# Stick-breaking weights without their last product: value differences in place of values

## The chip, the cores and the metric

One core of a Trainium2 chip runs the whole program: two decoder layers over 1024 tokens of width 1024, in float32. The metric is the device time of one execution in microseconds (us), as the median of several runs. PE is TensorE (matrix products and transposes), DVE is VectorE, ACT is ScalarE, POOL is GpSimd, and SP is the engine whose queue issues the DMAs here.

## The reference, cut to what matters

Each layer has three token mixers side by side (stick-breaking attention with 4 heads of 64, multi-head latent attention "MLA" with 4 heads, RWKV-7 with 8 heads), an output projection with a layer norm, and a gated convolutional feed-forward part (FFN). The change touches the first mixer alone:

```python
def stick_breaking_attention(q, k, v):
    scale = q.shape[-1] ** -0.5
    kpos = jnp.arange(s_len, dtype=jnp.int32)
    def block(qb, start):                      # 128 queries
        z = jnp.einsum('bhqd,bhkd->bhqk', qb, k).astype(jnp.float32) * scale
        qpos = start + jnp.arange(Q_BLOCK, dtype=jnp.int32)
        past = kpos[None, :] < qpos[:, None]
        log_keep = jnp.where(past, jax.nn.log_sigmoid(-z), 0.0)
        log_later = lax.cumsum(log_keep, axis=3, reverse=True) - log_keep
        w = jnp.where(past, jnp.exp(jax.nn.log_sigmoid(z) + log_later), 0.0)
        return jnp.einsum('bhqk,bhkd->bhqd', w.astype(v.dtype), v)
```

With b = sigmoid(z) and K[j] = the product of (1 - b) over all past keys from j on, the weight of key j is b[j] * K[j+1], which is K[j+1] - K[j].

## The kernel before, in words

The program is written with a tile framework. It emits instructions in program order with priorities (PRIORITY, lines 45 to 57); a list scheduler then fixes one static order for each engine and puts in the semaphores. A tile tag with `bufs=n` has n buffers in rotation, and a new tile of the tag waits until one of them is free. All DMAs are issued by SP, in their static order, so that one whose wait isn't over holds up those behind it.

A layer runs through these stages:

- `phase_a` (line 1075): the input projections of MLA and RWKV, the RWKV preparations, then the RWKV chain (`rw_chain`), a recurrence over 8 steps for each of two groups of heads. During the second group `proj_sb` (line 263) computes the six projections of the stick-breaking heads, two heads at a time: queries and keys of pair 0, queries and keys of pair 1, then values of pair 0 and of pair 1. After each of the six, `step` lets the chain emit one step more. Each projection is 48 matmuls, evicted by ACT into a tile "pst" (one tag with 4 buffers) and stored to DRAM (`sqd`, `skd`, `svd`). The values are transposed first, 128 by 128 (line 281), through PSUM tiles that the chain uses too (`ps2`: "pa", "py", "pq"), and copied by DVE (line 282) into another "pst" tile.
- The attention (lines 1191 to 1212): four MLA heads and four stick-breaking heads, as four generators whose blocks of 128 queries are interleaved by STREAM_ORDER. Pairs of heads are taken in turn; the second pair goes through its blocks from the longest to the shortest. Four MLA blocks are emitted ahead, before the pools of the chain close (line 1201). The queries and keys come back from DRAM into "pst" tiles (lines 359, 360, 533, 534) and are split into high and low parts.
- `oproj` (output projection, from the last query block to the first) and `ffn`.

A stick-breaking block over LL = 128 to 1024 keys (`stick_block`, `stick_post`): PE computes scores in one or two PSUM pieces (lines 388, 389), ACT takes the tanh (390), POOL fills the diagonal block with -1 where the key isn't past (396), DVE computes (1 - tanh)/2, the factors 1 - b (397), into one of three buffers `kp3` (the tags "LA", "T", "pd" of an earlier stage, cleared by POOL at line 1198), takes their running product from the right (399), and multiplies (1 + tanh) by that product (400). PE transposes the result (339), ACT evicts it (340), and when both heads of a pair have a block, PE multiplies it by the values (`attn_out`, 323), ACT evicts with the factor 0.5 (418), and SP stores it. An MLA block has its own chain of DVE and ACT instructions (maximum 562, 564, 566; exponential 567 on ACT; normalization 580, 582).

Of the kernel before, what the change touches and what calls it, by code (L numbers as in the profile page):

```python
# [69 lines left out]
class Body:  # L70
    def __init__(self, ctx, tc, a):
        self.ctx, self.tc, self.nc, self.a = ctx, tc, tc.nc, a
        self.n = 0
        self.ptags = {}
        self.rot = 0
        self.sq = 0
        self.sn = self.kn = 0
        self.pairs = {}
# [184 lines left out]
    def proj_sb(self, l, pool, step):  # L263
        nc, W = self.nc, self.a["w_in"][l]
        for j in range(2):
            for base, dst in ((SBQ, self.sqd), (SBK, self.skd)):
                hi, lo = self.wload(W, [(base + j * P, P)])
                d = self.t(pool, [P, S], "pst", bufs=4)
                self.proj_copy(hi, lo, d)
                nc.sync.dma_start(dst[j], d)  # L270
                step(4)
        for j in range(2):
            hi, lo = self.wload(W, [(SBV + j * P, P)])
            d = self.t(pool, [P, S], "pst", bufs=4)
            self.proj_copy(hi, lo, d)
            o = self.t(pool, [P, S], "pst", bufs=4)
            for q in range(2):
                pt = self.ps2()
                for i in range(4):
                    ii = 4 * q + i  # L280
                    nc.tensor.transpose(pt[:, i * P : i * P + P], d[:, ii * P : ii * P + P], self.ident)
                nc.vector.tensor_copy(o[:, q * 512 : q * 512 + 512], pt)
            step(4)
            nc.sync.dma_start(self.svd[j], o.rearrange("p (i v) -> p i v", v=P))

# [31 lines left out]

    def attn_out(self, wts, nb, V, av):
        ms = []
        for j in range(nb):  # L320
            for hp in range(2):
                hc = slice(hp * 64, hp * 64 + 64)
                ms.append(self.nc.tensor.matmul(av[hc], V[:, j, hc], wts[hp][:, j, :], start=j == 0, stop=j == nb - 1))
        self.in_order(ms)
# [18 lines left out]
    def stick(self, wp, ip, hp):  # L343
        for pr in range(2):
            if hp == 0:
                self.sv = self.t(wp, [P, NT, P], "mv")
                self.nc.sync.dma_start(self.sv, self.svd[pr])
            V = self.sv
            qk = self.stick_qk(wp, pr, hp)
            for i in range(NT)[:: 1 - 2 * pr]:  # L350
                self.stick_block(i, pr, hp, qk, V, wp, ip)
                yield

    def stick_qk(self, wp, pr, hp):
# [20 lines left out]
    def stick_block(self, i, pr, hp, qk, V, wp, ip):  # L375
# [6 lines left out]
        n = self.sn = self.sn + 1  # L382
        self.kn += 1
        kp = self.kp3[self.kn % 3]
        for u, (a0, a1) in enumerate(self.pieces(LL)):
# [4 lines left out]
            nc.scalar.activation(be[:, a0:a1], s, AF.Tanh, scale=0.0625)  # L390
        self.stick_post(be, kp, i, LL, nb, n, V, hp, pr, wp)

    def stick_post(self, be, kp, i, LL, nb, n, V, hp, pr, wp):
        nc = self.nc
        dg = be[:, i * P : LL]
        nc.gpsimd.affine_select(out=dg, in_=dg, pattern=[[-1, P]], base=0, channel_multiplier=1, compare_op=ALU.is_gt, fill=-1.0)
        nc.vector.tensor_scalar(kp[:, : LL - 1], be[:, 1:LL], -0.5, 0.5, op0=ALU.mult, op1=ALU.add)
        kv = kp[:, : LL - 1][:, ::-1]
        nc.vector.tensor_tensor_scan(kv, kv, self.ones.to_broadcast([P, LL - 1]), 1.0, op0=ALU.mult, op1=ALU.mult)
        nc.vector.scalar_tensor_tensor(be[:, :LL], be[:, :LL], 1.0, kp[:, :LL], op0=ALU.add, op1=ALU.mult)  # L400
        wt = self.w_transpose(self.wt4[:, n % 6], be, nb, "pa")
        self.pair(("s", pr, i), wt, hp, nb, V, self.mixd[pr], i, wp, "pa", 0.5)

# [8 lines left out]
    @prioritized  # L412
    def av_store(self, wts, nb, V, dst, i, wp, tag, sc):
        nc = self.nc
        av = self.pst(tag)[:, :P]
        self.attn_out(wts, nb, V, av)
        ot = self.t(wp, [P, P], "avo", bufs=2)
        nc.scalar.mul(ot, av, sc)
        nc.sync.dma_start(dst[:, i * P : i * P + P], ot)
# [150 lines left out]
    def mla_post(self, st, e, pcs, n, nb, sc, pr, hp, i, V, wp):  # L570
# [13 lines left out]
        wt = self.w_transpose(self.wt4[:, self.sn % 6], e, nb)  # L584
        self.pair(("m", pr, i), wt, hp, nb, V, self.mixd[2 + pr], i, wp, "av", 1.0)

# [559 lines left out]
    def run(self):  # L1146
# [5 lines left out]
        self.mqd, self.mkd = dd("mqd", [4, 96, S]), dd("mkd", [4, 96, S])  # L1152
        self.mvd, self.svd = dd("mvd", [2, P, NT, P]), dd("svd", [2, P, NT, P])
        self.sqd, self.skd = dd("sqd", [2, P, S]), dd("skd", [2, P, S])
# [20 lines left out]
        for l in range(L):  # L1175
# [15 lines left out]
            with ExitStack() as c:  # L1191
# [3 lines left out]
                self.wt4 = self.t(self.ip, [P, 6, NT, P], "Aa")  # L1195
                self.kp3 = [self.t(self.ip, [P, S], n) for n in ("LA", "T", "pd")]
                for t in self.kp3:
                    nc.gpsimd.memset(t, 0.0)
                for t in range(MLA_AHEAD):
# [58 lines left out]
```

## Time and profile before

| | |
|---|---|
| median of 3 runs (lowest to highest) | 3023.79 us (3023.44 to 3026.31) |
| the profiled execution, its own time | 3025.69 us |
| its span, first to last instruction | 3024.0 us |
| mean granted clock of TensorE | 0.989 |
| busy in the span: PE, DVE, ACT, POOL | 2913.1, 1727.8, 1074.8, 230.8 us |

The page divides the span into 40 equal slices of 75.6 us. Counted from 1, slices 8 and 9, 28 and 29 hold most of the attention of the two layers: DVE is busy 8 or 9 tenths there, and PE falls to 8 tenths in three of the four. In the slices of the FFN PE stands at 9 tenths or more and DVE at 3 to 5. A busy time of PE is made of modelled ends of pipelined matmuls, so it isn't PE at its peak; PEld, the loading of weights, is shown beside it. A row of the windows below gives start and end, the length, the busy time of PE, PEld, DVE, ACT and POOL with the number of instructions in brackets, the granted clock of TensorE as a share of full speed, the busy share of the DMA engines and what they moved in GB/s.

### The profile page before, as it was taken

To read this page: it belongs to the slowest core of one execution; us is meant where nothing else is said; L and a number is where in the kernel's file an instruction comes from. 1 tells how busy PE (TensorE), PEld (TensorE's weight loads), DVE (VectorE), ACT (ScalarE), POOL (GpSimd) and SP (SyncE) were. 2 spreads that over 40 slices of the span, in tenths; PEclk is the share of its full clock that TensorE was granted. 3 is DMA by queue.
4 is the path that set the end of the run, shared out by engine and by line. 5 is a ranking of instruction groups with operands and counts; after the bars stand their busy time and mean duration, and the time that the engine had idled before them with its cause. 6 is when DMAs were issued, how large, how long until landed. Compare 5 with 4: busy or idle time off the path is not lost.

```text
span 3024.0 us, 41845 instructions
## 1 busy us (share of the span) xinstructions
PE 2913.1 (96%) x16572; PEld 2322.0 (77%) x16572; DVE 1727.8 (57%) x2857; ACT 1074.8 (36%) x1833; POOL 230.8 (8%) x308
## 2 busy tenths in 40 slices
PE   8999999889999999999999999999899999999998
PEld 6777777667888888888877777776678888888887
DVE  4568665886544444344645677568965443434437
ACT  5454454762211112121254644457612111212120
POOL 0001122030000000000000011210300000000000
PEclk9999999999999999999999999999999999999999
DMA  4353666324411111111124446562244111111111
GB/s 135 91 157 102 209 193 203 92 82 137 167 56 42 42 43 55 49 56 49 63 77 125 127 133 207 177 213 66 90 145 163 42 42 42 56 49 55 50 49 56
DMA packets 338260, 301.78 MB, mean 100 GB/s; under 512 B 24200, under 2 KB 302992, under 8 KB 338064
## 3 DMA queue, kind: packets, MB, share of 16 engines
q1 hardware_dynamic: 338064, 299.11, 32.6%
q8 instruction: 131, 2.15, 0.3%
q14 instruction: 65, 0.53, 0.1%
HBM read 208.87 MB, written 90.18 MB: 99 GB/s over the span
## 4 chain that ended last, share of the span: by engine, by line
PE 76%; DVE 10%; issue 8%; ACT 3%; DMA 3%; POOL 1%; SPq 0%; POOLq 0%; DVEq 0%; ACTq 0%
PE psmm L207 16%; PE psmm L206 16%; PE psmm L205 16%; PE psps L205 5%; PE psps L206 5%; PE psps L207 5%; PE pspa L848 2%; DVE pd L731 1%; PE pspi L792 1%; PE psmt L216 1%; DMA LA<-xxd 1%; DVE T L732 1%; PE pspa L684 1%; ACT pd L726 0%; DVE mexp L400 0%
## 5 line engine op out<-in xcount | busy, mean ns | idle before, releaser
L207 PE MATMUL psmm<-xTh,wlo 128*128 128x512 f32 x2144 | 849.1, 396 | 0.0
L205 PE MATMUL psmm<-xTh,whi 128*128 128x512 f32 x2144 | 847.0, 395 | 0.0
L206 PE MATMUL psmm<-xTl,whi 128*128 128x512 f32 x2144 | 846.8, 395 | 0.0
L200 ACT CAST whi<-raw 128x1024 fp32r<-128x1024 f32 x152 | 160.0, 1053 | 1062.1 <-PE psmm L206 1048.6
L205 PEld LDWEIGHTS psmm<-xTh,whi 128*128 128x128 f32 x2144 | 404.0, 189 | 88.6 <-issue 6.1
L206 PEld LDWEIGHTS psmm<-xTl,whi 128*128 128x128 f32 x2144 | 404.2, 189 | 87.9 <-issue 4.6
L207 PEld LDWEIGHTS psmm<-xTh,wlo 128*128 128x128 f32 x2144 | 404.2, 189 | 87.6 <-issue 4.2
L201 DVE TENSOR_TENSOR wlo<-raw,whi 128x1024 fp32r<-128x1024 f32 x152 | 185.6, 1221 | 456.7 <-ACT whi L200 440.4
L1060 DVE TENSOR_TENSOR y<-y,psps 128x512 f32<-128x512 f32 x288 | 196.5, 687 | 171.1 <-PE psps L207 171.0
L205 PE MATMUL psps<-wdh,hh 128*128 128x512 f32 x672 | 266.7, 397 | 0.0
L206 PE MATMUL psps<-wdl,hh 128*128 128x512 f32 x672 | 262.9, 391 | 0.0
L207 PE MATMUL psps<-wdh,hl 128*128 128x512 f32 x672 | 259.6, 391 | 0.0
L205 PEld LDWEIGHTS psps<-wdh,hh 128*128 128x128 f32 x672 | 126.1, 188 | 36.8 <-ACT hh L200 5.9
L923 POOL TENSOR_TENSOR lsm<-lsm,small 128x1 f32<-128x1 f32 x32 | 29.3, 915 | 1629.9 <-DVE lsm L922 1629.9
L207 PEld LDWEIGHTS psps<-wdh,hl 128*128 128x128 f32 x672 | 126.2, 188 | 26.9
L206 PEld LDWEIGHTS psps<-wdl,hh 128*128 128x128 f32 x672 | 126.2, 188 | 25.4
L1035 DVE TENSOR_TENSOR cv<-cv,psmm 128x1024 f32<-128x1024 f32 x44 | 53.8, 1222 | 136.6 <-PE psmm L207 131.7
L201 DVE TENSOR_TENSOR wdl<-raw,wdh 128x1024 fp32r<-128x1024 f32 x42 | 51.5, 1226 | 88.2 <-ACT wdh L200 88.2
L1030 ACT ACTIVATE cv<-cv 128x1024 f32<-128x1024 f32 x44 | 46.7, 1061 | 115.8 <-DVE cv L1029 115.8
L848 PE MATMUL pspa<-RBl,PSl 128*128 128x128 f32 x512 | 72.0, 286 | 11.1 <-ACT QC L851 5.3
L848 PEld LDWEIGHTS pspa<-RBl,PSl 128*128 128x128 f32 x512 | 64.6, 195 | 19.3 <-ACT QC L851 8.3
L206 PE MATMUL psmm<-wol,whi 128*128 128x512 f32 x192 | 76.6, 399 | 1.6 <-DVE wol L201 1.6
(444 smaller groups left out, 4504.7 us busy)
## 6 DMA issues: line engine op xcount, KB each, us to landing
raw<-in_ffn_w_up_dram SPq DMA_DIRECT2D x88, 512.0 KB
raw<-in_w_in_dram SPq DMA_DIRECT2D x44, 512.0 KB
raw<-in_ffn_w_down_dram SPq DMA_DIRECT2D x44, 512.0 KB
rbd<-RB SPq DMA_DIRECT2D x64, 256.0 KB
PSl<-psd SPq DMA_DIRECT2D x32, 512.0 KB
RBl<-rbd SPq DMA_DIRECT2D x32, 512.0 KB
psd<-Vz SPq DMA_DIRECT2D x64, 128.0 KB
xxd<-X SPq DMA_DIRECT2D x64, 128.0 KB
```

Source lines behind the costliest of these rows:

```text
L200: self.nc.scalar.copy(hi, src)
L201: (eng or self.nc.vector).tensor_tensor(lo, src, hi.bitcast(F32), op=ALU.subtract)
L205: mm(out, lh, rh, start=start, stop=False)
L206: mm(out, lh, rl, start=False, stop=False)
L207: mm(out, ll, rh, start=False, stop=stop)
L216: nc.tensor.transpose(pt[:, k * P : k * P + P], xt[:, kk * P : kk * P + P], self.ident)
L684: ms.append(nc.tensor.matmul(pAs[h][:, cc * P : cc * P + P], flat(BK[hr, 2 * g + cc // 2, cc % 2]), AR[hr, :, 2 * g + cc // 2, cc % 2, :], ...
L731: mul = lambda o, x, y: nc.vector.tensor_tensor(o, x, y, op=ALU.mult)
L848: nc.tensor.matmul(pQ[:, f, e, :], PSh[:, f, h, e, :], RBh[:, f, h, e, :], start=True, stop=True)
L1030: nc.scalar.activation(cv, cv, AF.Gelu)
L1035: nc.vector.tensor_tensor(cv, cv, pg, op=ALU.mult)
L1060: nc.vector.tensor_tensor(y[:, i, hs], y[:, i, hs], ps, op=ALU.add)
```

## The change

The sum over keys of (K[j+1] - K[j]) v[j] is summed by parts: it is the sum of K[j] (v[j-1] - v[j]) and a last term. So the running product itself becomes the weight, and the values are replaced by differences of neighbours.

- In `stick_post` the product of line 400 goes, and the factors and the running product are computed in place in the tile of the tanh, over LL columns instead of LL - 1. The three buffers `kp3` and their clearing go. The eviction's factor 0.5 goes too.
- `proj_sb` projects queries, keys and values of a pair in turn. Of the values it forms e[t] = v[t-1] - v[t] (two DVE instructions), transposes and stores it (`store_v`: 8 transposes, 2 DVE copies, 1 DMA), overwrites the last column of each block of 128 keys with v[t-1] (one DVE copy of 8 columns), and transposes and stores that as well. So a pair takes four "pst" tiles for its values instead of two.
- In the attention the last key block of a query block takes its values from the second array (`Vd`), all others from the first. Both are loaded, pair 0 into the tags "LA" and "T", pair 1 into "pd" and a new tile "mdd"; the two "mv" tiles of that pool go.

```diff
-        for j in range(2):
             hi, lo = self.wload(W, [(SBV + j * P, P)])
             d = self.t(pool, [P, S], "pst", bufs=4)
             self.proj_copy(hi, lo, d)
-            o = self.t(pool, [P, S], "pst", bufs=4)
-            for q in range(2):
-                pt = self.ps2()
-                for i in range(4):
-                    ii = 4 * q + i
-                    nc.tensor.transpose(pt[:, i * P : i * P + P], d[:, ii * P : ii * P + P], self.ident)
-                nc.vector.tensor_copy(o[:, q * 512 : q * 512 + 512], pt)
-            step(4)
-            nc.sync.dma_start(self.svd[j], o.rearrange("p (i v) -> p i v", v=P))
+            e = self.t(pool, [P, S], "pst", bufs=4)
+            nc.vector.tensor_tensor(e[:, 1:S], d[:, 0 : S - 1], d[:, 1:S], op=ALU.subtract)
+            nc.vector.tensor_scalar(e[:, 0:1], d[:, 0:1], -1.0, None, op0=ALU.mult)
+            self.store_v(e, self.svd[0, j], pool)
+            nc.vector.tensor_copy(e[:, P - 1 : S : P], d[:, P - 2 : S : P])
+            self.store_v(e, self.svd[1, j], pool)
+            step(2)
+
+    def store_v(self, e, dst, pool):
+        nc = self.nc
+        o = self.t(pool, [P, S], "pst", bufs=4)
+        for q in range(2):
+            pt = self.ps2()
+            for i in range(4):
+                ii = 4 * q + i
+                nc.tensor.transpose(pt[:, i * P : i * P + P], e[:, ii * P : ii * P + P], self.ident)
+            nc.vector.tensor_copy(o[:, q * 512 : q * 512 + 512], pt)
+        nc.sync.dma_start(dst, o.rearrange("p (i v) -> p i v", v=P))
...
-                ms.append(self.nc.tensor.matmul(av[hc], V[:, j, hc], wts[hp][:, j, :], start=j == 0, stop=j == nb - 1))
+                ms.append(self.nc.tensor.matmul(av[hc], (Vd if j == nb - 1 else V)[:, j, hc], wts[hp][:, j, :], start=j == 0, stop=j == nb - 1))
...
-                self.sv = self.t(wp, [P, NT, P], "mv")
-                self.nc.sync.dma_start(self.sv, self.svd[pr])
+                self.sv = self.stick_steps(wp, pr)
...
+    def stick_steps(self, wp, pr):
+        r3 = lambda t: t.rearrange("p (j v) -> p j v", v=P)
+        if pr:
+            V = r3(self.t(self.ip, [P, S], "pd")), self.t(wp, [P, NT, P], "mdd", bufs=1)
+        else:
+            V = tuple(r3(self.t(self.ip, [P, S], n)) for n in ("LA", "T"))
+        for u in range(2):
+            self.nc.sync.dma_start(V[u], self.svd[u, pr])
+        return V
...
-        nc.vector.tensor_scalar(kp[:, : LL - 1], be[:, 1:LL], -0.5, 0.5, op0=ALU.mult, op1=ALU.add)
-        kv = kp[:, : LL - 1][:, ::-1]
-        nc.vector.tensor_tensor_scan(kv, kv, self.ones.to_broadcast([P, LL - 1]), 1.0, op0=ALU.mult, op1=ALU.mult)
-        nc.vector.scalar_tensor_tensor(be[:, :LL], be[:, :LL], 1.0, kp[:, :LL], op0=ALU.add, op1=ALU.mult)
+        nc.vector.tensor_scalar(be[:, :LL], be[:, :LL], -0.5, 0.5, op0=ALU.mult, op1=ALU.add)
+        kv = be[:, :LL][:, ::-1]
+        nc.vector.tensor_tensor_scan(kv, kv, self.ones.to_broadcast([P, LL]), 1.0, op0=ALU.mult, op1=ALU.mult)
...
-        nc.scalar.mul(ot, av, sc)
+        nc.scalar.copy(ot, av)
...
-                self.kp3 = [self.t(self.ip, [P, S], n) for n in ("LA", "T", "pd")]
-                for t in self.kp3:
-                    nc.gpsimd.memset(t, 0.0)
```

## Rows read from the trace of the kernel before

**Rows 1.** Windows, attention of each layer, then FFN: start:end, us, busy times by engine.
```profile
545.00:695.00 150.00, 129.34 (x1033) 99.15 (x1034) 136.37 (x257) 103.08 (x262) 32.18 (x47) 0.97 0.25 72
2050.00:2200.00 150.00, 131.33 (x1028) 99.43 (x1023) 131.94 (x247) 103.08 (x262) 33.65 (x47) 0.97 0.25 73
1000.00:1100.00 100.00, 100.00 (x441) 82.13 (x440) 43.83 (x44) 24.48 (x24) 0.00 (x0) 1.00 0.20 58
```

**Rows 2.** Windows of line 400 alone, attention of both layers: DVE busy (instructions).
```profile
525.00:700.00 175.00, 24.25 (x32) 0.97 0.30 87
2030.00:2215.00 185.00, 25.14 (x32) 0.96 0.32 94
```

**Rows 3.** Timeline of DVE, one stick-breaking block of 1024 keys: start, duration, line.
```profile
641.95 0.69 DVE L397 TENSOR_SCALAR LA<-mexp 128x1023 f32<-128x1023 f32 x1
642.67 2.29 DVE L399 TENSOR_TENSOR_SCAN LA<-LA,small 128x1023 f32<-128x1023 f32 x1
644.99 1.23 DVE L400 SCALAR_TENSOR_TENSOR mexp<-mexp,LA 128x1024 f32<-128x1024 f32 x1
```

**Rows 4.** Waits of PE, 545 to 695, then 2050 to 2200: total us, times, longest.
```profile
PE pspa L339 <- DVE mexp L400: 8.3, 12, 1.5
PE pspa L339 <- DVE mst L566: 3.5, 3, 2.1
PE psav L339 <- DVE mexp L580: 3.4, 6, 0.8
...
PE psav L339 <- DVE mexp L580: 5.0, 5, 2.7
PE pspa L339 <- DVE mst L566: 2.6, 2, 2.3
PE pspa L339 <- DVE mexp L400: 1.9, 4, 0.8
PE psav L339 <- DVE mexp L582: 1.7, 4, 0.7
```

**Rows 5.** Windows of 10 us around the end of the projections, columns as rows 1.
```profile
490.00:500.00 10.00, 10.00 (x98) 7.84 (x98) 6.49 (x19) 3.22 (x7) 1.76 (x2) 1.00 0.72 243
500.00:510.00 10.00, 7.31 (x63) 6.08 (x61) 5.52 (x12) 5.09 (x10) 2.32 (x4) 1.00 0.74 229
510.00:520.00 10.00, 6.71 (x69) 5.43 (x68) 8.72 (x22) 7.33 (x12) 1.13 (x2) 0.89 0.84 216
```

**Rows 6.** Timeline of SP's queue after the last projection: start, duration, line.
```profile
500.25 0.32 SPq L530 DMA_DIRECT2D mv<-mvd  x1
500.62 0.42 SPq L533 DMA_DIRECT2D pst<-mqd  x1
503.51 0.33 SPq L284 DMA_DIRECT2D svd<-pst  x1
...
506.39 0.41 SPq L534 DMA_DIRECT2D pst<-mkd  x1
...
510.86 0.38 SPq L534 DMA_DIRECT2D pst<-mkd  x1
```

**Rows 7.** Timeline, all engines, around the last projection: operations like the added ones.
```profile
487.31 0.17 DVE L887 TENSOR_SCALAR vs<-vs 128x4 f32<-128x4 f32 x1
...
493.49 0.66 PE L281 MATMUL pspq<-ident,pst 128*128 128x128 f32 x4
...
494.85 0.69 DVE L282 COPY pst<-pspq 128x512 f32<-128x512 f32 x1
...
508.57 1.22 DVE L373 TENSOR_TENSOR ql<-pst,qh 96x1024 fp32r<-96x1024 f32 x1
```

**Rows 8.** Chain that ended last, 490 to 735: start, us, what.
```profile
500.62 4.08 DMA pst<-mqd
```

**Rows 9.** The tile of the values: count, ns min/median/max, first and last start.
```profile
L323 PE MATMUL pspa<-Aa,mv x576: 272/273/477, 549.5 to 2196.1; 128*64 128x128 f32 x192
...
L347 SPq DMA_DIRECT2D mv<-svd x4: 320/378/431, 536.9 to 2039.2; - x4
```

More of the change, by code (lines that the diff above doesn't have):

```diff
@@ L76, in __init__ @@
         self.sq = 0
-        self.sn = self.kn = 0
+        self.sn = 0
         self.pairs = {}
@@ L316, in in_order, with attn_out @@
             self.tc.add_manual_dep(b.ins, a.ins.name, mybir.DependencyInfo(mybir.DependencyClass.NoSync, mybir.DependencyReason.DATA), reason="array halves take turns")
-    def attn_out(self, wts, nb, V, av):
+    def attn_out(self, wts, nb, V, Vd, av):
         ms = []
@@ L382, in stick_block @@
         n = self.sn = self.sn + 1
-        self.kn += 1
-        kp = self.kp3[self.kn % 3]
         for u, (a0, a1) in enumerate(self.pieces(LL)):
@@ L390, in stick_block, with stick_post @@
             nc.scalar.activation(be[:, a0:a1], s, AF.Tanh, scale=0.0625)
-        self.stick_post(be, kp, i, LL, nb, n, V, hp, pr, wp)
-    def stick_post(self, be, kp, i, LL, nb, n, V, hp, pr, wp):
+        self.stick_post(be, i, LL, nb, n, V, hp, pr, wp)
+    def stick_post(self, be, i, LL, nb, n, V, hp, pr, wp):
         nc = self.nc
@@ L396, in stick_post @@
         nc.gpsimd.affine_select(out=dg, in_=dg, pattern=[[-1, P]], base=0, channel_multiplier=1, compare_op=ALU.is_gt, fill=-1.0)
-        nc.vector.tensor_scalar(kp[:, : LL - 1], be[:, 1:LL], -0.5, 0.5, op0=ALU.mult, op1=ALU.add)
-        kv = kp[:, : LL - 1][:, ::-1]
-        nc.vector.tensor_tensor_scan(kv, kv, self.ones.to_broadcast([P, LL - 1]), 1.0, op0=ALU.mult, op1=ALU.mult)
-        nc.vector.scalar_tensor_tensor(be[:, :LL], be[:, :LL], 1.0, kp[:, :LL], op0=ALU.add, op1=ALU.mult)
+        nc.vector.tensor_scalar(be[:, :LL], be[:, :LL], -0.5, 0.5, op0=ALU.mult, op1=ALU.add)
+        kv = be[:, :LL][:, ::-1]
+        nc.vector.tensor_tensor_scan(kv, kv, self.ones.to_broadcast([P, LL]), 1.0, op0=ALU.mult, op1=ALU.mult)
         wt = self.w_transpose(self.wt4[:, n % 6], be, nb, "pa")
-        self.pair(("s", pr, i), wt, hp, nb, V, self.mixd[pr], i, wp, "pa", 0.5)
+        self.pair(("s", pr, i), wt, hp, nb, *V, self.mixd[pr], i, wp, "pa")
     def pair(self, key, wt, hp, *args):
@@ L412, in av_store @@
     @prioritized
-    def av_store(self, wts, nb, V, dst, i, wp, tag, sc):
+    def av_store(self, wts, nb, V, Vd, dst, i, wp, tag):
         nc = self.nc
         av = self.pst(tag)[:, :P]
-        self.attn_out(wts, nb, V, av)
+        self.attn_out(wts, nb, V, Vd, av)
         ot = self.t(wp, [P, P], "avo", bufs=2)
-        nc.scalar.mul(ot, av, sc)
+        nc.scalar.copy(ot, av)
         nc.sync.dma_start(dst[:, i * P : i * P + P], ot)
@@ L584, in mla_post @@
         wt = self.w_transpose(self.wt4[:, self.sn % 6], e, nb)
-        self.pair(("m", pr, i), wt, hp, nb, V, self.mixd[2 + pr], i, wp, "av", 1.0)
+        self.pair(("m", pr, i), wt, hp, nb, V, V, self.mixd[2 + pr], i, wp, "av")
     def q2(self, tp):
@@ L1152, in run @@
         self.mqd, self.mkd = dd("mqd", [4, 96, S]), dd("mkd", [4, 96, S])
-        self.mvd, self.svd = dd("mvd", [2, P, NT, P]), dd("svd", [2, P, NT, P])
+        self.mvd, self.svd = dd("mvd", [2, P, NT, P]), dd("svd", [2, 2, P, NT, P])
         self.sqd, self.skd = dd("sqd", [2, P, S]), dd("skd", [2, P, S])
```

## Prediction

> **What bounds the kernel now.** I read the table of the 40 slices first: PE is full nearly everywhere except in the two attention stretches, so only these, and the handover into them, can give or lose anything. Then the windows. In 150 us of the attention of each layer DVE is busy 136.4 and 131.9 us, PE 129.3 and 131.3, ACT 103.1, POOL 32 to 34 [rows 1]. DVE and PE both look close to full, so the question is which of them is the limit. The waits of PE answer it: the longest are all ended by DVE, 8.3 + 3.5 + 3.4 = 15.2 us in the first layer and 5.0 + 2.6 + 1.9 + 1.7 = 11.2 us in the second, 26.4 us in all [rows 4], out of 150 - 129.3 = 20.7 and 150 - 131.3 = 18.7 us in which PE isn't busy [rows 1]. So DVE sets the pace and PE follows it. The reader is to see there too that only 8.3 + 1.9 us of these waits end with line 400 itself; the others end with MLA's instructions, which queue behind stick-breaking work on the same DVE.
>
> How much room PE has is less plain. Its weight loads are busy 99.2 and 99.4 us of 150, while in an FFN stretch with a PE that never stops they are busy 82.1 of 100 [rows 1]. Most of the attention's matmuls are small, and a short gap hides behind the modelled end of the one before. The Trainium skill (Perfetto Trace Analysis, section Identifying the Most-Contended Engine) says that matmul busy time is a bad measure of headroom and weight-load time a good one: by the page PE's work here would fit into 99.2/0.821 = 121 us, an estimate, so that PE would not stop a gain before DVE's whole relief is used up; by matmul busy time PE could give back no more than its 39.4 idle us. That is rival B below, and its chance is taken from the rows alone: the rows on either reading leave 39 us or more.
>
> **The change, part by part.**
>
> *The product of line 400 goes.* It costs DVE 24.25 us in the first layer and 25.14 in the second, 32 instructions each [rows 2], 49.4 us in all. In a block of 1024 keys it is 1.23 of 0.69 + 2.29 + 1.23 = 4.21 us [rows 3], so a block also reaches its transposes that much sooner. The two instructions that stay run over one more column: the scan goes at 2.29 us for 1023, so 64 blocks cost some 0.1 us together, and working in place adds no data. I take that as nothing. What is that worth? Upper bound: DVE stays the limit with as much idle time as now, 49.4 us. Lower bound: only the waits that end with line 400 itself vanish, 10.2 us [rows 4]. I take the waits of PE that DVE ends, 26.4 us: with 24 to 25 us less in each window DVE would be at 112.1 of 150 us in the first layer and 106.8 in the second, below PE's 129 to 131, and late next would be ACT (103.1) and PE itself, with the transposes waiting for ACT's evictions. A shorter window than 150 - 13 = 137 us would ask for ACT and DVE to be busy at 75 to 82% side by side in an order fixed beforehand; DVE alone manages 88 to 91% now.
>
> *Twice the transposes of values.* 16 more per layer. Four take 0.66 us, and DVE's copy out of PSUM 0.69 [rows 7]. The stretch in which they lie has PE busy 10.00 of 10 [rows 5], so PE pays for all of them: at (0.66 - 0.27)/3 = 0.13 us each (0.27 is the latency of the last, by the minimum for such a size in rows 9), 2.1 us per layer, 4.2 in all.
>
> *DVE in the projections.* Per layer two subtractions of 1024 columns at 1.22 us (the nearest row is a subtraction of 1024 columns), four more copies at 0.69, and four instructions of 1 or 8 columns at about 0.17 [rows 7]: 2.4 + 2.8 + 0.7 = 5.9 us. DVE is busy 6.5 of 10 there [rows 5], with PE full beside it, so that the first pair's half is hidden. Without that cover it would be 3 us per layer. The second pair's half lies in the handover.
>
> *The handover.* After the last projection PE drops to 7.3 and 6.7 of 10 [rows 5]: the tail of the RWKV chain and MLA's first loads run one behind the other. The first loads of MLA are issued when the projections are done with their input: 500.25 and 500.62, the store of the last values at 503.51, the first head's keys at 506.39, the second head's at 510.86 [rows 6]. They go into "pst" tiles, of which there are four, and after the change the last values take all four (d, e and two transposed copies). The first MLA load must then wait until d is free: until the subtraction (1.22), 8 transposes (1.3) with a copy (0.69) and the strided copy (0.17) are done, some 3.4 us, so 504 in place of 500.6. The second waits for the other 8 transposes, about 2 us later; the last two wait for the two stores to land. The first head's keys are late already now at 506.39, so the first score moves by less than the first load does. The added waits stand in SP's queue, with the chain's loads and the stores of the mixers behind them, and in DVE's (the strided copy waits for 8 transposes, and the chain's state updates queue behind it). Bounds: 0 (the chain's tail hides it) and 11.8 us per layer (rival D); I take 2 us, near the lower end, because three of the four loads are already issued 6 to 10 us after the projections. 4.0 us in all.
>
> *The rest.* Two arrays of values are loaded per pair in place of one. Now the load is issued at 536.9 and first used at 549.5 [rows 9], and a load takes about 4.1 us [rows 8], so two more fit; pair 0 can be loaded long before. Uncovered it would be 4 us per layer. The order of the projections changes nothing in their sum, and the chain gets the same six steps. The clearing of `kp3` was on POOL, which is busy 1.8 to 2.3 of 10 [rows 5]. The number of matmuls in the attention, ACT's evictions and the transposes of the weights stay.
>
> **Sum.** 26.4 gained, 4.2 + 4.0 = 8.2 lost: 18.2 us less. The profiled execution took 3025.7 us (its span 3024.0), 1.9 above the median of 3023.8; 3025.7 - 18.2 = 3007.5, and on the median 3005.6, so I say 3006.
>
> **The rivals.**
>
> A, the forecast, 3006, with a range of its own of 2994 to 3020 (gain 18 to 34 us, cost 4 to 14).
>
> B, DVE stays the limit to the end, and the whole 49.4 us comes back less 8.2: 2983. For it: PE's weight loads leave room, and the second half of each stretch, with the long blocks of pair 1, is nearly DVE's alone. Against it: ACT at 103 of 150 and chains that pass through POOL, DVE, PE and ACT with two or three buffers each.
>
> C, the relief is swallowed: PE, ACT and the fixed order give back only the 10.2 us that end with line 400, and 8.2 are lost: 3022, no change that can be measured (0.2%, 6 us, is about what a measurement of this kernel can tell). For it: in the second layer line 400 ends only 1.9 us of PE's waits. Against it: the others end with DVE as well.
>
> D, slower: the four "pst" tiles. If MLA's first load is put behind the second store of the last values in SP's order, it waits until that store has landed: 503.5 + 1.2 + 0.2 + 8 transposes, two copies and their turns on PE (about 3.4) = 508.3, and 4.1 for landing [rows 6 to 8]: 512.4 in place of 500.6, 11.8 us per layer with nothing else for PE to do. It decides from 11.1 us per layer at A's gain, and from 3 us at C's. With a gain midway, 18.3, it is 18.3 - 23.6 - 4.2 = 9.5 us slower: 3033. The Trainium skill (Perfetto Trace Analysis, section Optimization Strategy) warns that bubbles that come back in a stretch can mean too few buffers for the next tile; by it D would show at the second pair's projections as well. No row shows such a bubble now, and a projection of 48 matmuls takes 10.9 us (441 per 100 us [rows 1]), which covers the stores in between.
>
> **How the numbers follow.** A 0.50, B 0.18, C 0.18, D 0.14. The predicted time is A's. The range goes from 2985, where most of B is left out, to 3030, where C is in and the worse half of D is out. Faster by over 0.2%: nearly all of A (0.47), all of B (0.18), a little of C (0.04), 0.69. Within 0.2%: 0.03 of A, 0.11 of C, 0.01 of D, 0.15. Slower: the rest, 0.16.
>
> **What would show it.** Right: no product on DVE; DVE at 80 to 85% of the attention's window, which is some 13 us shorter per layer; waits of PE for DVE down to a half or less; ACT's evictions as the next releaser. B would show DVE still at 90%, C a window of the same length with DVE idle a quarter of it. For the handover: the first load of MLA queries 3 to 4 us after the last projection, and PE's first score 2 us later than now; D would show it 12 us after. The sum is wrong above all if the scheduler orders the interleaved blocks differently enough to move other waits, or if PE's small matmuls have less room than their weight loads suggest.

## The result, and the profile after

The changed kernel takes 3050.36 us (median, 3049.51 to 3054.57); the kernel before, measured beside it, 3024.61. The ratio is 1.0087, with a 95% interval of 1.0070 to 1.0105: 25.7 us slower, outside the predicted range. The product is gone and DVE did get lighter (1696.7 us busy; it was 1727.8), but the loss lies elsewhere. The line of busy times of the page after:

```profile
PE 2926.0 (96%) x16604; PEld 2336.2 (77%) x16604; DVE 1696.7 (56%) x2813; ACT 1073.3 (35%) x1833; POOL 229.5 (8%) x302
```

Three landmarks in each timeline cut a layer into parts: the last eviction of a projection (line 253), MLA's first maximum (line 562, after: 576), and the last eviction of stick-breaking's product with the values (418, after: 432). They start at

| us | layer 1 | layer 2 |
|---|---|---|
| before | 500.3, 515.4, 697.0 | 2002.6, 2017.6, 2196.4 |
| after | 519.2, 538.8, 711.9 | 2034.2, 2052.5, 2221.2 |

- Up to the end of the projections: +18.9 us, and from layer 1's last landmark on +16.7. In sum **+35.6**.
- The handover, from there to MLA's first maximum: 15.1 became 19.6, and 15.0 became 18.3. In sum **+7.8**.
- The attention: 181.6 became 173.1, and 178.8 became 168.7. In sum **-18.6**.

That makes +24.8, close to the slowdown of 25.7 us by the medians. So the projections lost twice as much as the attention seems to gain; how much of that is gain, the experiments tell.

**Where the projections lose it.** Windows around the end of the projections, first of after, then of before (columns as in rows 1):

```profile
460.00:470.00 10.00, 3.71 (x17) 3.64 (x17) 0.75 (x2) 0.58 (x1) 0.00 (x0) 0.60 0.43 137
470.00:480.00 10.00, 7.96 (x75) 6.86 (x75) 5.44 (x16) 3.11 (x7) 0.00 (x0) 0.89 0.70 237
480.00:490.00 10.00, 7.42 (x57) 6.17 (x57) 5.23 (x15) 2.44 (x5) 2.03 (x2) 0.66 0.68 234
```
```profile
460.00:480.00 20.00, 20.00 (x165) 16.94 (x163) 8.21 (x25) 5.26 (x11) 1.86 (x2) 1.00 0.67 229
```

Before, PE is full for the whole stretch. After, it is busy 3.71 of 10 us, and the granted clock falls to 0.60, near the lower of its two levels (1.2 of 2.4 GHz), so what work there is goes slower as well: below, four transposes (L290) take 0.66 us at 479.83 and 1.12 us at 483.98. The timeline of PE after shows the hole (start, duration, line; in brackets the idle time before and what ended it):

```profile
459.23 0.39 PE L207 MATMUL psmm<-xTh,wlo 128*128 128x512 f32 x1
466.29 5.63 PE L862 MATMUL pspa<-RBl,PSl 128*128 128x128 f32 x24 [6.67 <-DMA PSl<-psd]
...
479.83 0.66 PE L290 MATMUL pspa<-ident,pst 128*128 128x128 f32 x4 [0.46 <-ACT QC L865]
...
483.98 1.12 PE L290 MATMUL pspq<-ident,pst 128*128 128x128 f32 x4 [0.46 <-ACT ys L898]
```

and the timeline of ACT after the evictions of projections next to it:

```profile
419.17 0.59 ACT L253 COPY pst<-psmm 128x512 f32<-128x512 f32 x1
...
486.01 1.07 ACT L253 COPY pst<-psmm 128x512 f32<-128x512 f32 x2 [1.64 <-DVE pst L279]
```

The second half of pair 0's values is evicted at 419.17, but the first of their transposes (L290) runs at 479.83. The last projection matmul before the hole ends at 459.6, and the next eviction of a projection comes at 486.01, released by the strided copy (L279) that frees the tile of the values. In between PE waits for the chain's load `PSl<-psd`. Before, it had projections to do during that load; now the projections stand too.

**The attention.** Windows of after, and PE's waits in the same two windows (total, times, longest):

```profile
567.00:712.00 145.00, 129.74 (x1034) 100.84 (x1035) 115.18 (x225) 102.80 (x265) 31.81 (x47) 0.94 0.26 77
2080.00:2221.00 141.00, 125.68 (x1035) 98.34 (x1034) 114.72 (x222) 102.08 (x263) 36.02 (x47) 0.98 0.27 78
```
```profile
PE pspa L347 <- DVE mexp L414: 3.9, 4, 1.9
PE pspa L347 <- DVE mst L580: 3.7, 4, 1.0
PE psav L347 <- DVE mexp L594: 1.6, 3, 0.7
...
PE psav L347 <- DVE mexp L594: 5.9, 4, 2.6
PE pspa L347 <- DVE mst L580: 2.8, 3, 1.5
PE pssc L205 <- ACT mexp L581: 2.0, 3, 0.8
```

DVE is busy 79 and 81% (forecast 80 to 85). Most of the waits that DVE ends did not go: line 414, the scan, stands where line 400 stood [rows 4], and MLA's normalization (594) still makes PE wait 5.9 us.

**The handover.** SP's queue after the last projection:

```profile
523.42 0.32 SPq L292 DMA_DIRECT2D svd<-pst  x1
524.18 0.33 SPq L547 DMA_DIRECT2D pst<-mqd  x1
530.06 0.31 SPq L548 DMA_DIRECT2D pst<-mkd  x1
530.78 0.33 SPq L292 DMA_DIRECT2D svd<-pst  x1
```

Before, MLA's first load followed the start of the last eviction by 0.4 us [rows 6]; now by 5.0 us, behind the first store of the last values. That is the place that the prediction named, at a price between its 3.4 and rival D's 11.8.

### The profile page after: what moved, and what is told of

It reads as the page before. It is cut to its first block, busy times and chain, and to the rows that moved or that the text cites. A ratio compares the mean times of both kernels' runs of the same rounds, so it can differ in the third digit from the quotient of the medians.

```text
span 3047.8 us, 41883 instructions
## 1 busy us (share of the span) xinstructions
PE 2926.0 (96%) x16604; PEld 2336.2 (77%) x16604; DVE 1696.7 (56%) x2813; ACT 1073.3 (35%) x1833; POOL 229.5 (8%) x302
## 4 chain that ended last, share of the span: by engine, by line
PE 76%; DVE 9%; issue 8%; DMA 3%; ACT 3%; POOL 1%; SPq 0%; POOLq 0%; DVEq 0%; ACTq 0%
PE psmm L207 16%; PE psmm L205 16%; PE psmm L206 16%; PE psps L205 5%; PE psps L206 5%; PE psps L207 5%; PE pspa L862 2%; DVE pd L745 1%; PE pspi L806 1%; PE psmt L216 1%; DMA LA<-xxd 1%; DVE T L746 1%; DVE mexp L414 1%; PE pspa L698 1%; ACT pd L740 0%
## 5 line engine op out<-in xcount | busy, mean ns | idle before, releaser
L862 PE MATMUL pspa<-RBl,PSl 128*128 128x128 f32 x512 | 79.0, 308 | 20.5 <-DMA PSl<-psd 13.4
L862 PEld LDWEIGHTS pspa<-RBl,PSl 128*128 128x128 f32 x512 | 71.5, 215 | 29.4 <-issue 16.4
L414 DVE TENSOR_TENSOR_SCAN mexp<-mexp,small 128x128 f32<-128x128 f32 (+7 forms) x64 | 87.9, 1377 | 0.7
```

The source lines that it names most:

```text
L862: nc.tensor.matmul(pQ[:, f, e, :], PSh[:, f, h, e, :], RBh[:, f, h, e, :], start=True, stop=True)
```

## The experiments: which part costs the time

Four kernels take the change apart. The first puts the values of both pairs back behind all queries and keys, the second makes only that move on the kernel before, and the last two carry only the new attention or only the new projections.

```diff
 # order alone, on the kernel before
                 step(4)
-        for j in range(2):
             hi, lo = self.wload(W, [(SBV + j * P, P)])
```

> The changed kernel with the projections in the order of before (queries and keys of both pairs, then the values of both pairs); all else as changed. Theory T (tiles): in turn, the first pair's values hold their four pst tiles until PE reaches their transposes, which stand behind the chain's wait for its loads, so the next pair's projections can't be evicted and PE runs empty for some 25 us per layer. In the old order no projection but the last values stands behind them, so most of the loss goes: 3010 to 3030 us. Rival W (work): the doubled transposes, copies and stores cost what they cost wherever they stand: 3045 to 3055 us. Rival M: the hole moves to the second pair's values, which now need the tiles of the first: 3030 to 3045 us.

> The kernel before with one edit: queries, keys and values of a pair are projected in turn; values are stored once, in two pst tiles a pair. Theory T: two tiles stay free for the next pair's queries and keys, so nothing is held up: 3018 to 3030 us. Rival O (order): the order alone opens the hole, since the transposes stand behind the chain's loads in any case: 3040 to 3055 us.

> The attention of the changed kernel behind the projections of the kernel before: values are stored once, undifferenced, and that array is loaded for both value arrays, so the stick-breaking outputs are those of other values. It measures the relief of DVE alone. From the two traces (first MLA score to last eviction of the attention 8.5 and 10.1 us shorter): 3005 us. If the relief is what the prediction took, 26 us: 2998 us. If DVE stays the limit to the end, 49 us: 2975 us. If the shorter attention is only a late start caught up, 3020 us or more.

> The projections of the changed kernel (in turn, differences, two stores a pair) in front of the attention of the kernel before, which multiplies by the differences as if they were values, so the stick-breaking outputs are others. It measures the cost alone. Theory T and the traces (last projection 18.9 us later in layer 0, first MLA score 23 us later): 2 x 20 to 24 us, 3064 to 3072 us. If the loss sits in the attention instead: 3030 us or less.

| kernel | median, us | ratio to before [95%] |
|---|---|---|
| before, with the order in turn (e2) | 3058.51 | 1.0116 [1.0101, 1.0131] |
| before, with the new projections (e4) | 3065.44 | 1.0139 [1.0124, 1.0154] |
| after | 3050.36 | 1.0087 [1.0070, 1.0105] |
| after, with the old order (e1) | 3019.68 | 0.9984 [0.9974, 0.9993] |
| before, with the new attention (e3) | 3013.74 | 0.9970 [0.9960, 0.9980] |

The order alone costs 35 us, with one value tile per pair transposed as ever. The theory that the loss needs the four tiles of the changed values falls with that; rival O holds, 3 us beyond its range. The extra transposes, copies and stores cost about 6 us (e1 against e3; e4 against e2 gives 7). The new attention brings 10 us (e3 against before), where 26.4 were forecast and e3's own expectation, from the landmarks, was 3005. The three nearly account for the result: 3024 + 35 + 6 - 10 = 3055, against 3050 measured. In the changed kernel itself the order costs 31 us (after against e1).

So not all of the 18.6 us that the landmarks give to the attention is gain: the handover and the attention together are only 10.8 us shorter. That a longer handover lets the chain's last steps and the first loads finish ahead of the first landmark is likely and not shown.

## The experiments: why the order costs it

Two links were suspected between a pair's values and the next pair's queries. The transposes of values take their PSUM tiles from the chain's three tags, in program order, so behind chain steps that wait for `psd`. And the next pair's queries take the next "pst" tile in rotation, behind those of the transposed values. Each kernel cuts one link and leaves the order in turn.

```diff
 # e5: a tag of its own for transposed values
-        o = self.t(pool, [P, S], "pst", bufs=4)
+        o = self.t(self.tl, [P, S], "vo", bufs=1)
 # e9: transposes through the projections' PSUM tag
-            pt = self.ps2()
+            pt = self.mm_ps()
```

> The changed kernel, in turn, with one edit: the transposed values go into a tile of their own tag instead of the rotation pst. The order alone, with two tiles a pair, cost 35 us, so the number of tiles isn't it. Theory R (rotation): tiles of one tag are handed out in program order, so the second pair's queries get none before the first pair's transposed values have theirs, and these wait for transposes that PE reaches only behind the chain. With a tag of their own nobody queues behind them: 3010 to 3028 us. Rival P: the values themselves (d and e) stay pinned all the same and the second pair's values run into them: 3035 to 3050 us.

> The changed kernel, in turn, with one edit: the transposes of values go through the PSUM tiles of the projections (three, tag mm) instead of those shared with the RWKV chain (pa, py, pq). Both R and P need the transposes to be late. If they are late because their PSUM tiles come behind those of chain steps that wait for the inversion, they now follow their projection at once, and the hole goes: 3010 to 3028 us. If PE's order or the tiles in SBUF alone make it: 3040 us or more.

They took 3031.11 us (ratio 1.0020 [1.0011, 1.0030], e5) and 3029.04 us (1.0016 [1.0006, 1.0025], e9), so each gives back 19 to 21 of the 31 us, and each ends a little above the 3010 to 3028 us that its theory forecast. The windows of PE in e5, then e9 (PE alone, then the clock and the DMA engines):

```profile
460.00:480.00 20.00, 19.84 (x140) 1.00 0.69 234
480.00:500.00 20.00, 19.35 (x179) 1.00 0.69 232
```
```profile
460.00:480.00 20.00, 18.96 (x143) 1.00 0.84 279
480.00:500.00 20.00, 20.00 (x199) 1.00 0.77 249
```

The hole is filled in both. So the hole takes both links: transposes that stand behind the chain, and tiles handed out behind the transposes. What e5 doesn't give back is at the handover, which grew to 29.4 and 23.1 us: MLA's first load goes out 12 us after the last eviction. Why is open; the copies into the one tile that now serves all four transposed arrays wait for it only 1.8 us in the whole program. In e9 the projections still lose 7.6 us in the first layer and 11.5 in the second, and the handover takes 20.5 us in each.

In e2 the queries of pair 1 get the buffer of the queries of pair 0, which had long been stored. Still their eviction comes late. The timeline of ACT in e2:

```profile
467.94 0.58 ACT L850 COPY QC<-pspa 64x512 f32<-64x512 f32 x1 [11.02 <-DVE QC L849]
...
484.56 1.06 ACT L253 COPY pst<-psmm 128x512 f32<-128x512 f32 x2
```

The eviction at 484.56 waited for nothing (no bracket). It stood behind the chain's copies in ACT's fixed order, the first of which had waited 11.02 us. So at this eviction a lack of free tiles isn't what e2 suffers from. That the scheduler hands out tiles of a tag strictly in program order, and puts the eviction late for that reason, is the likeliest reading and only argued.

## The experiments: what a lighter DVE gives back

Two kernels go further than the new attention in one direction each: without the scan, and with only the first and the last key block in the products with the values, of all heads. A third moves the subtraction that gives the low parts of pair 1's queries and keys (line 382) from POOL, where it goes in four pieces, to DVE, where it goes in one. (The expectations of e16 and e19 below call this a split of the long blocks; the edit is the same as here.) All three load undifferenced values, as e3 does, and the first two leave out work besides, so their outputs are not those of the reference.

```diff
 # e11, on e3
-        nc.vector.tensor_tensor_scan(kv, kv, self.ones.to_broadcast([P, LL]), 1.0, op0=ALU.mult, op1=ALU.mult)
 # e12, on e3
+            if j not in (0, nb - 1):
+                continue
 # e10, on e3
-SPLIT_STICK = (0, 4)
+SPLIT_STICK = (0, 0)
```

> As the attention of the changed kernel behind the projections of the kernel before (3013.7 us), and the running product of DVE is left out too, so the stick-breaking weights are the factors alone: another 43 us less for DVE per layer. If DVE still sets the pace of the attention: 2935 to 2975 us. If it no longer does, and the relief stopped short because something else is the limit: 2998 to 3014 us.

> As the attention of the changed kernel behind the projections of the kernel before (3013.7 us), and of the products with the values only the first and the last key block are computed, in MLA and stick-breaking, so their outputs are partial sums: 30 of 72 instructions of a pair's eight blocks stay, some 20 us less work for PE per layer. If PE now sets the pace: 2970 to 2985 us. If DVE or the chains between the engines do: 3003 to 3014 us.

> The same edit (low parts of the second pair on DVE) on the changed attention behind the old projections (3013.7 us), where stick-breaking outputs are those of undifferenced values. Theory S: 3004 to 3010 us. Rival: 3013 to 3022 us.

Without the scan: 2976.71 us (0.9840 [0.9826, 0.9855] of before), 37 us less than e3, for 79 us less of DVE's busy time on the page (1607.3, e3 1686.7). With 672 matmuls fewer: 2989.26 us (0.9883 [0.9865, 0.9901]), 24.5 us less, for 32 us less of PE's (2873.1, e3 2905.2). Windows of the attention, e11 and then e12:

```profile
520.00:670.00 150.00, 142.22 (x1175) 112.38 (x1174) 91.56 (x248) 117.95 (x312) 27.90 (x53) 0.98 0.35 102
```
```profile
520.00:670.00 150.00, 129.06 (x817) 94.93 (x816) 126.58 (x272) 117.97 (x310) 35.77 (x52) 0.96 0.34 99
```

With DVE at 61%, PE is busy 142 of 150 us: there PE is close to full. With PE lightened, DVE stands at 84%. Neither engine alone sets the pace, and both times lie between the two ranges that their expectations named. Of the 49 us of line 400 some 20% came back (e3), of the next 79 us of DVE 47%, of the 32 us of PE 76%. These shares can't be read from the waits. PE's waits that DVE ends, all of them, add up to 28.9 us before and to 26.4 in e3, in the two windows of [rows 4]; the longest in e3, first layer, then second:

```profile
PE pspa L339 <- DVE mexp L406: 5.8, 5, 3.7
PE psav L339 <- DVE mexp L586: 2.8, 2, 2.2
PE pspa L339 <- DVE mst L572: 1.5, 2, 0.9
...
PE psav L339 <- DVE mexp L586: 5.8, 5, 2.6
PE pspa L339 <- DVE mst L572: 2.6, 2, 1.5
PE pspa L339 <- DVE mexp L406: 2.1, 4, 0.9
```

The waits that ended with line 400 now mostly end with the scan (406): 7.9 us in place of 10.2. Taking out the product brought 10 us, about what ended with it; taking out the scan brought 37, almost five times what ended with it.

What DVE meets first when it gets lighter is its own block's chain: the groups of its first instruction in a block (busy, mean ns, then the idle time before it and what ended it), of before and then of e3:

```profile
L397 DVE TENSOR_SCALAR T<-mexp 128x127 f32<-128x127 f32 (+7 forms) x22 | 10.3, 468 | 2.6 <-POOL mexp L396 2.6
L397 DVE TENSOR_SCALAR pd<-mexp 128x383 f32<-128x383 f32 (+7 forms) x21 | 10.1, 482 | 1.8 <-POOL mexp L396 1.6
L397 DVE TENSOR_SCALAR LA<-mexp 128x255 f32<-128x255 f32 (+7 forms) x21 | 9.7, 462 | 4.8 <-POOL mexp L396 4.6
```
```profile
L404 DVE TENSOR_SCALAR mexp<-mexp 128x128 f32<-128x128 f32 (+7 forms) x64 | 30.0, 471 | 24.2 <-POOL mexp L403 23.2
```

DVE now sits idle for 24.2 us, before 2.6 + 1.8 + 4.8 = 9.2, until POOL has masked the diagonal block; POOL in turn comes behind ACT and PE's scores, and behind its own work on the low parts.

With the low parts on DVE (e10): 3009.96 us (0.9951 [0.9934, 0.9967]), 3.8 us less than e3, at the edge of theory S's range. Where the pairs change, e3 and then e10:

```profile
625.00:635.00 10.00, 5.50 (x21) 4.30 (x22) 8.68 (x12) 3.56 (x8) 9.96 (x8) 0.64 0.31 99
```
```profile
625.00:635.00 10.00, 7.08 (x45) 5.42 (x46) 9.86 (x18) 6.84 (x15) 1.36 (x1) 0.83 0.28 89
```

In e3 POOL is busy 9.96 of 10 us with the low parts of pair 1's queries (line 382), and PE waits 2.5 us for it. Those pieces stood ahead of the masks too: in e10 the wait of DVE's first instruction for the mask is half as long.

```profile
L404 DVE TENSOR_SCALAR mexp<-mexp 128x128 f32<-128x128 f32 (+7 forms) x64 | 29.3, 460 | 12.2 <-POOL mexp L403 11.4
```

Whether the DVE of before, with the product still on it, could have taken that work was not run.

## The experiments: fewer tiles at the handover, and an unforeseen cost

In the old order the handover was 25.9 and 21.5 us (e1) against 15.1 and 18.1 (e3). In its first layer the condition of rival D holds: MLA's first load stands right behind the second store of the last values, 12.5 us after the last eviction (498.92). SP's queue there:

```profile
511.07 0.32 SPq L293 DMA_DIRECT2D svd<-pst  x1
511.44 0.42 SPq L548 DMA_DIRECT2D pst<-mqd  x1
```

In its second layer the load stands behind the first of these stores, 5.2 us after the eviction. To see whether the four tiles make the difference, the second array was reduced: it differs from the first in one row only, so that row is transposed and stored by itself and loaded over the copy. That takes three tiles (e6), or two with the difference formed in place (e13; e14 with the low parts on DVE as in e10). The loads of all three:

```diff
-        for u in range(2):
-            self.nc.sync.dma_start(V[u], self.svd[u, pr])
+        self.nc.sync.dma_start(V[0], self.svd[pr])
+        self.nc.sync.dma_start(V[1][0 : P - 1], self.svd[pr][0 : P - 1])
+        self.nc.sync.dma_start(V[1][P - 1 : P], self.svb[pr][None])
```

> The changed kernel with the projections in the old order, and without the second set of transposes: the second value array differs from the first only in the last key of each block, so these 8 columns are transposed by one small transpose and stored as a row (4 KB), and the second array is loaded from both. A pair's values take three pst tiles (d, e, one transposed copy) instead of four. In the old order with four tiles (3019.7 us) the last projection is on time, but MLA's first score comes 25.9 and 21.5 us behind it instead of 15.0. Theory H (handover): the late score is the wait of MLA's loads for the values' tiles; with three it comes 16 to 20 us behind, and the time is 3012 to 3017 us. Rival X: it is the extra transposes and copies in the tail of the chain: the same 3012 to 3017 us, but then two tiles (next kernel) are no better than three.

> As the kernel with the row, and the difference is formed in place, from the last token to the first, after the 8 columns have been saved: two pst tiles a pair as before the change, 2 subtractions, 6 small instructions and 2 small transposes a layer more. Theory H: MLA's first score 15 to 17 us behind the last projection, 3008 to 3015 us, about the time of the changed attention behind the old projections (3013.7 us). Rival X: no better than with three tiles. If the handover is set by neither: 3018 us or more.

> As the in-place kernel, and the low parts of the second pair's queries and keys (line 373, some 17 us per layer on POOL) are computed on DVE, 4 subtractions of 1.22 us per layer. Theory S: after the relief the attention has a bubble at the change of pairs that POOL makes (PE waits 2.5 us for it, and its clock falls to 0.64), and DVE now has room: 4 to 10 us less than the in-place kernel. Rival: DVE still sets the pace there, and 5 us more on it cost as much as the bubble: the same or up to 8 us more.

All three take longer than before: 3053.58 us (1.0097 [1.0082, 1.0112]), 3065.26 (1.0135 [1.0120, 1.0151]) and 3059.51 (1.0116 [1.0100, 1.0133]). The handover did shrink, to 20.1 us in each layer of e6 (the 19.5 of an expectation below doesn't fit these landmarks), but right behind it PE was busy 8.42 of 20 us. The load of 127 of 128 partitions was suspected. One kernel changes that alone on e3, and three put a whole load in its place.

```diff
 # e18, on e3
-        for u in range(2):
-            self.nc.sync.dma_start(V[u], self.svd[pr])
+        self.nc.sync.dma_start(V[0], self.svd[pr])
+        self.nc.sync.dma_start(V[1][0 : P - 1], self.svd[pr][0 : P - 1])
+        self.nc.sync.dma_start(V[1][P - 1 : P], self.svd[pr][P - 1 : P])
 # e15 (on e13), e16 (on e14), e17 (on e6)
-        self.nc.sync.dma_start(V[1][0 : P - 1], self.svd[pr][0 : P - 1])
+        self.nc.sync.dma_start(V[1], self.svd[pr])
```

> The kernel with the attention of after and the projections of before (it loads the same values twice, so the boundary row is left out), 3013.7 us, with one change: the second array of values is loaded as 127 partitions and one, from the same stored data. Theory Q: the crawl comes with this load alone, 3040 to 3055 us, and PE has idle stretches after MLA's first blocks. Rival R: the split costs one more DMA and no time, 3012 to 3016 us.

> Old order of projections, three stick tiles for a pair's values, boundary row stored by itself, second array loaded whole and its last partition overwritten. The same kernel with a load of 127 partitions took 3053.6 us, with 20.1 and 19.5 us between the last projection and MLA's first score (25.9 and 21.5 with four tiles, at 3019.7 us). Theory Q: 3011 to 3016 us, that is the four-tile kernel less the 7.8 us of the handover. Rival R: 3045 us or more.

> The in-place kernel again (all queries and keys first, two stick tiles for a pair's values, the boundary row stored by itself), except that the second array of values is loaded whole, 128 partitions, and its last partition is overwritten afterwards; before, 127 partitions and one partition were loaded apart. Theory Q: the load of 127 partitions was what made the transfers crawl after the handover, so all of that goes: 3008 to 3016 us, with the handover between the last projection and MLA's first score at 20 us or less. Rival R: the crawl has another cause (the order of the loads, the extra transpose, the in-place subtraction), and this stays above 3045 us.

> As the run with the whole load, and the long stick-breaking blocks are no longer split between DVE and POOL (that by itself brought 4 us). Theory Q: 3004 to 3012 us, the shortest so far. Rival R: above 3045 us.

| kernel | median, us | ratio to before [95%] |
|---|---|---|
| e3 with 127 rows and one (e18) | 3053.55 | 1.0094 [1.0080, 1.0108] |
| three tiles, whole load (e17) | 3014.02 | 0.9966 [0.9952, 0.9980] |
| two tiles, whole load (e15) | 3031.55 | 1.0021 [1.0011, 1.0030] |
| two tiles, whole load, low parts on DVE (e16) | 3027.35 | 1.0010 [1.0001, 1.0019] |

The load alone costs 40 us (e18 against e3), and taking it out returns 40 (e6 to e17), 34 (e13 to e15) and 32 (e14 to e16). Theory Q on the cause holds; the two kernels with two tiles stay some 15 us above the times that it gave them. SP's queue in e18, then three windows of e18, then the same stretches of e3:

```profile
513.96 10.57 SPq L361 DMA_DIRECT2D T<-svd  x1
...
525.84 0.53 SPq L917 DMA_DIRECT2D mixd<-mo  x1
```
```profile
520.00:525.00 5.00, 5.00 (x32) 4.76 (x33) 3.36 (x16) 1.40 (x6) 1.42 (x2) 0.50 0.07 27
...
530.00:535.00 5.00, 0.25 (x3) 0.05 (x1) 0.00 (x0) 0.00 (x0) 0.00 (x0) 0.70 0.19 63
535.00:540.00 5.00, 0.00 (x0) 0.00 (x0) 0.00 (x0) 0.00 (x0) 0.00 (x0) 0.50 0.06 26
```
```profile
520.00:525.00 5.00, 4.56 (x35) 4.35 (x35) 3.80 (x17) 2.20 (x9) 1.88 (x2) 0.69 0.51 133
...
530.00:535.00 5.00, 4.16 (x25) 2.81 (x25) 4.01 (x14) 2.81 (x10) 0.72 (x1) 1.00 0.46 128
535.00:540.00 5.00, 4.68 (x38) 3.40 (x38) 2.95 (x8) 4.72 (x13) 0.00 (x0) 1.00 0.52 141
```

In e18 the DMA engines are busy 0.06 to 0.07 of the time and move 26 to 27 GB/s, which is one engine's work out of 16. SP's queue stands for 10.57 us at the one-row load that follows the load of 127. The store `mixd<-mo` takes 15.84 us in the chain of work that ended last, and ACT, which needs the tile `mo` again, waits for it:

```profile
525.84 15.84 DMA mixd<-mo
...
541.76 0.81 ACT L914 ACTIVATE mo<-pspa,pv 128x128 f32<-128x128 f32 x2 [13.62 <-DMA mixd<-mo]
```

MLA's exponentials stand behind that instruction in ACT's order, and PE's scores behind them. That the store is late because it shares the one engine with the load is argued, not shown.

The Trainium skill (DMA: Bandwidth & Descriptors, section Why a DMA increments its semaphore by 16 and not by 1) gives the rule: a transfer is spread over the largest number of engines up to 16 that divides its slowest dimension, which for 127 partitions is one. The rows of e18 agree, at a sixteenth of the engines.

On the tiles: with three instead of four the handover goes from 25.9 to 20.1 us in the first layer and from 21.5 to 20.1 in the second (e17), MLA's first load from 12.5 to 5.1 us after the last eviction in the first, and the time from 3019.7 to 3014.0, that of e3. But e17 also drops the second set of transposes and copies, and two tiles shorten the handover no further (20.7 and 19.8 us, e15), which is what rival X said of these extra transposes. So whether tiles or transposes make the late load is not settled. The two-tile kernel is 17 us slower than the three-tile one; why is open.

The best of these kernels was run with the low parts on DVE as well:

> The fastest kernel so far that keeps the old order of projections and takes three stick tiles for a pair's values (3014.0 us), with the long stick-breaking blocks no longer split between DVE and POOL. That step brought 3.8 us on the kernel with the attention of after and the old projections, and 4.2 us on the kernel with two tiles. If it adds up: 3008 to 3012 us. If DVE needs POOL's help as soon as the handover is longer: 3014 or more.

It takes 3007.65 us, just below the range for steps that add up, and 0.9944 [0.9931, 0.9958] of before: 18 us less than before by the medians of that comparison (3025.73), 43 us less than after. The low parts on DVE are worth 3.8 to 6.4 us in the four pairs of kernels that differ in that alone (e3 and e10, e13 and e14, e15 and e16, e17 and e19). The attention of e19 lasts 167.8 and 168.4 us, from 181.6 and 178.8.

## Why the prediction was wrong

- **The step that failed** is "The order of the projections changes nothing in their sum", with "a projection of 48 matmuls takes 10.9 us" and "which covers the stores in between". The prediction looked only at stores in between. It didn't ask what the transposes themselves queue behind: PSUM tiles of the chain, which waits for loads in its turn. The order was priced at nothing and the transposes at 4.2 us; the projections lost 35.6, and the order alone costs 35 (e2). In the old order all four projections of queries and keys lie ahead of the values and fill PE while the chain waits; in turn, the first pair's values sit in the middle of that stretch.
- **Rival D** had the right kind of cause (tiles that come free late) at the wrong place. Its sentence on the rule of the Trainium skill (Perfetto Trace Analysis, section Optimization Strategy), that by it the bubble would show at the second pair's projections, is what happened, though in e2 the late eviction waited for no buffer. The rival got a chance of 0.14, for no row of before shows such a bubble. Rows of before could not: there the dependence lay behind work that covered it. Where D itself put the cost, at MLA's first load, its condition came true in the old order, in the first layer of e1, where the handover is 10.8 us longer than before (D said 11.8).
- **The gain** was mis-sized. It was taken as 26.4 us, all of PE's waits that DVE ends [rows 4]; the new attention alone brought 10 (e3), and those waits hardly shrank (28.9 to 26.4 us). That 10 us are also rival C's number, the 10.2 that end with line 400 itself, is luck as far as the runs go: the same rule gives the scan 7.9 us, and it was worth 37 (e11). The premise "DVE sets the pace and PE follows it" is too strong: without the scan PE filled up (e11), and with the product alone gone DVE waited for POOL's mask. The landmark that was to confirm the gain (a window 13 us shorter per layer; measured 8.5 and 10.1) is not a gain by itself, since the handover ahead of it grew by 4.5 and 3.3.
- **The handover** was taken as 2 us a layer and measured 4.5 and 3.3. The mechanism was right, the wait of MLA's first load for a tile [rows 6], in after for the one that the strided copy (line 279) frees; the first load came 5.0 us after the last eviction rather than 3 to 4.
- **The extra transposes, DVE work and handover** were taken as 8.2 us together and came to 6 in the old order (e1 against e3).
- **Right**: DVE's share (79 and 81%), and that the extra transposes, copies and stores by themselves are cheap. Loading two arrays of values per pair was taken as nothing; e3 does it and still gains 10, but no run prices it alone.

## What to carry to other kernels

When a change reorders producers that share a rotation of tiles with a slow chain, list for each moved step every queue and every tile tag that it draws from, and what stands ahead of it there; work that only filled a wait has no row of its own in the profile, and its cover is missed only once it is gone. The waits that end with an instruction don't tell what its removal is worth: here they gave 10.2 us for the product, which brought 10, and 7.9 for the scan, which brought 37. A kernel that only leaves the instruction out tells it before the change is written. A load of 127 partitions is better made whole, with the odd row overwritten.

## What the runs showed of the hardware

- A load of 127 partitions went at the pace of one of 16 DMA engines, 26 to 27 GB/s with the engines busy 0.06 to 0.07, and four such loads (one per pair and layer) cost 40 us. A whole load with a second DMA for the odd row cost nothing that shows (e17 3014.0 us, e3 3013.7).
- When PE starved, the clock fell: 0.60 in the hole of after, where PE was busy 3.71 of 10 us, and 0.50 in e18 at 535 to 540 us, behind 5 us with PE busy 0.25. Of the 18.9 us in the first layer, the three windows of after show 10.9 us of PE's idle time; what the lower clock and the extra transposes make of the rest was not measured apart.
